# Who issues one plain weight transfer: GpSimd behind another one, or ACT

## The chip, the cores and the metric

The kernel runs on one core of one Trainium2 chip. The metric is the device time of one execution in microseconds (us): the median of several runs. Beside the timed runs there is one profiled execution, from which every row below comes; times in rows count from the start of its span.

## The reference

One decoder layer on a sequence of 512 tokens of width 1024, in float32: a SwiGLU half, a mixing block (a gated linear recurrence with 4 heads, and a gated short convolution), cross-attention into 256 memory rows, a second SwiGLU half and a last norm.

```
def swiglu(h, w_gate, w_up, w_down):
    return (jax.nn.silu(h @ w_gate) * (h @ w_up)) @ w_down
...
x = x + 0.5 * swiglu(rms_norm(x, ffn1_norm[l]), ffn1_gate[l], ffn1_up[l], ffn1_down[l])
...
x = x + 0.5 * swiglu(rms_norm(x, ffn2_norm[l]), ffn2_gate[l], ffn2_up[l], ffn2_down[l])
return rms_norm(x, final_norm)
```

The inner width of a SwiGLU half is 2816. The change touches only the products with w_gate and w_up, in both halves.

## The kernel before

Every float32 product is made of three: each operand is split into a high part, rounded for the fast multiply, and a low part, the rest. So each weight tile that comes from memory is first cast by ACT (`whi`, lines 100 and 312) and then subtracted by VectorE (`wlo`, lines 101 and 313), and TensorE (PE) multiplies high by high, high by low and low by high.

A SwiGLU half (class Half, used as f1 and f2) makes its 22 tiles of 128 inner columns in two ways. Tiles 0 to 3 (CLASSIC is 4) are made with plain products. From tile 4 on, tiles are made in pairs: gate and up weights of two tiles and the two halves of the input features and of the tokens form 2 x 2 blocks, and seven products take the place of eight (function seven). In the program's order the products are p1, p5, r6, p2, r7, p4, p3. The first three matter here. p1 multiplies the weight block b11 by the input block a11 into the PSUM tile psA. p5 multiplies t1 by q1 into psD. r6 first adds b22 to t1 (line 355), casts and splits that sum, and multiplies it by n2, on top of psA. Then p2 multiplies b21 into psB. Each of the products is 24 matmuls of 256 columns.

The five weight tiles of a pair are brought by load (line 287). Three are plain: b11, b22, b21. Two are sums of two blocks of the weights, made by the transfers themselves: t1 is first written plainly (line 300) and then a second transfer, which only GpSimd can issue, adds to it (line 301); t3 in the same way (lines 302 and 304). The adding transfer waits until the plain one has landed. All the tiles come from one pool of six buffers (tag raw), which the steps that prepare the inputs use too, so a transfer also waits until the last reader of its buffer is done. For t1 of the first pair that is n2l, the low part of n2 of the first tile pair (line 237).

The first pair (m equal to CLASSIC, once in each half) is loaded early, while the plain products' down projection (down_pairs, line 441) runs: line 466. There b11 goes out on GpSimd, t1's plain transfer on ACT and t3's plain transfer on SP; in later pairs b11 and t1 go out on SP and t3 on GpSimd.

The order of instructions on each engine isn't written out by hand: a scheduler takes the program, gives each instruction a place by its own estimate of when it could run, and then fixes one order for each engine. Each engine runs its list in order; GpSimd, SP and ACT issue transfers at the place where these stand in their list, and wait there for what the transfer needs.

In rows the names lose their ends: b_f is b11, b22 or b21; t_f is t1 or t3 (and a temporary of line 220); in_w is the weights; q1, n2, a11 with h or l are the parts of the inputs.

Of the kernel before, what the change touches and what calls it, by code (L numbers as in the profile page):

```python
# [38 lines left out]
def decoder_layer(ctx: ExitStack, tc: tile.TileContext, xT, memT, vecs, masks, ident_d,  # L39
                  w1, w1d, w_in, w_i, w_out, w_q, w_k, w_v, w_o, w2, w2d, gfin, out):  # L40
    nc = tc.nc
# [142 lines left out]
    CLASSIC = 4  # L184
    PARTS = ((0, 4), (4, 10), (10, 16), (16, FT))

    class Half:
# [99 lines left out]
        def load(self, m):  # L287


            def tile(key):  # L290
                return self.hp.tile([P, 2, 512], F32, tag="raw", name=f"{key}_{self.name}{m}", bufs=6)

            def src(j, h):
                return self.wgu[m:m + 2, j, :, h * 512:(h + 1) * 512].rearrange("m p c -> p m c")

            b11, t1, t3, b22, b21 = (tile(k) for k in ("b11", "t1", "t3", "b22", "b21"))

            queue = nc.gpsimd if m == CLASSIC else nc.sync
            queue.dma_start(b11, src(0, 0))
            (nc.scalar if m == CLASSIC else nc.sync).dma_start(t1, src(0, 0))  # L300
            nc.gpsimd.dma_start(t1, src(1, 0), accum_op=ALU.add)
            (nc.sync if m == CLASSIC else nc.gpsimd).dma_start(t3, src(1, 0))
            nc.sync.dma_start(b22, src(1, 1))
            nc.gpsimd.dma_start(t3, src(1, 1), accum_op=ALU.add)
            nc.sync.dma_start(b21, src(0, 1))
            return dict(b11=b11, t1=t1, b22=b22, b21=b21, t3=t3)
# [177 lines left out]
    with tc.tile_pool(name="start", bufs=1, reuse_waits="tile") as sp:  # L484
# [6 lines left out]
        for k0, k1 in steps:  # L491
            c = slice(k0 * P, k1 * P)
            src = w1[:2, :, :, c].rearrange("m j p c -> p (m j) c")
# [660 lines left out]
```

## Time and profile before

| | us |
|---|---|
| median of 3 runs | 1110.08 (1109.69 to 1110.9) |
| profiled execution | 1112.6 |
| its span, first to last instruction | 1110.8 |
| PE busy | 1093.6 (98%) |
| VectorE busy | 731.0 (66%) |
| ACT busy | 485.5 (44%) |
| GpSimd busy | 76.3 (7%) |

The busy time of an engine tells which engine the others have to keep fed; the waits tell where it wasn't. In a timeline row the first number is the start, the second the duration, and the bracket at the end holds the idle time of the engine before this instruction and what ended it. PE's matmuls overlap: the distance between starts is what one costs.

### The profile page before, as it was taken

To read this page: it belongs to the slowest core of one execution; us is meant where nothing else is said; L and a number is where in the kernel's file an instruction comes from. 1 tells how busy PE (TensorE), PEld (TensorE's weight loads), DVE (VectorE), ACT (ScalarE), POOL (GpSimd) and SP (SyncE) were. 2 spreads that over 40 slices of the span, in tenths; PEclk is the share of its full clock that TensorE was granted. 3 is DMA by queue.
4 is the path that set the end of the run, shared out by engine and by line. 5 is a ranking of instruction groups with operands and counts; after the bars stand their busy time and mean duration, and the time that the engine had idled before them with its cause. 6 is when DMAs were issued, how large, how long until landed. Compare 5 with 4: busy or idle time off the path is not lost. (4 is left out here: it accounts for less than half of the span.)

```text
span 1110.8 us, 15932 instructions
## 1 busy us (share of the span) xinstructions
PE 1093.6 (98%) x6522; PEld 978.4 (88%) x6522; DVE 731.0 (66%) x975; ACT 485.5 (44%) x662; POOL 76.3 (7%) x77
## 2 busy tenths in 40 slices
PE   7989999999999999999999999999999999999997
PEld 6879998998998888888889888888899989989995
DVE  6696755774667575885777556548967747755744
ACT  6344533552445343222454344435535524533553
POOL 1011100110100000000100000000011101100102
PEclk9999999999999999999999999999999999999999
DMA  6266664673623322322233424232757645755421
GB/s 232 74 186 184 180 165 124 172 172 109 172 52 107 107 95 68 104 76 86 67 114 114 134 78 124 83 95 76 200 149 180 168 124 133 201 152 154 96 76 76
DMA packets 69177, 140.53 MB, mean 127 GB/s; under 512 B 4880, under 2 KB 21264, under 8 KB 69104
## 3 DMA queue, kind: packets, MB, share of 16 engines
q1 hardware_dynamic: 53760, 105.92, 30.4%
q0 software_dynamic: 12944, 30.28, 13.6%
q10 hardware_dynamic: 2400, 3.31, 0.9%
q8 instruction: 51, 0.84, 0.3%
q14 instruction: 22, 0.18, 0.1%
HBM read 137.40 MB, written 2.10 MB: 126 GB/s over the span
## 5 line engine op out<-in xcount | busy, mean ns | idle before, releaser
L100 ACT ACTIVATE whi<-raw 128x1024 fp32r<-128x1024 f32 (+1 forms) x133 | 133.1, 1002 | 302.5 <-issue 68.7
L101 DVE TENSOR_TENSOR wlo<-raw,whi 128x1024 fp32r<-128x1024 f32 (+1 forms) x133 | 152.9, 1151 | 66.5 <-ACT whi L100 66.0
L312 ACT ACTIVATE whi<-b_f 128x1024 fp32r<-128x1024 f32 x72 | 76.4, 1061 | 111.9 <-issue 36.0
L313 DVE TENSOR_TENSOR wlo<-b_f,whi 128x1024 fp32r<-128x1024 f32 x72 | 88.2, 1224 | 44.9 <-ACT whi L312 43.5
L109 PE MATMUL psd_f<-al_f,whi 128*128 128x512 f32 x280 | 109.1, 390 | 0.0
L110 PE MATMUL psd_f<-ah_f,wlo 128*128 128x512 f32 x280 | 108.9, 389 | 0.0
L108 PE MATMUL psd_f<-ah_f,whi 128*128 128x512 f32 x280 | 108.3, 389 | 0.0
L313 DVE TENSOR_TENSOR wlo<-t_f,whi 128x1024 fp32r<-128x1024 f32 x54 | 66.1, 1224 | 40.3 <-ACT whi L312 40.3
L181 DVE SCALAR_TENSOR_TENSOR xall<-psd_f,xall 128x512 f32<-128x512 f32 x52 | 35.5, 690 | 76.5 <-PE psd_f L110 76.5
L312 ACT ACTIVATE whi<-t_f 128x1024 fp32r<-128x1024 f32 x54 | 57.0, 1056 | 55.8 <-issue 23.7
L110 PEld LDWEIGHTS psd_f<-ah_f,wlo 128*128 128x128 f32 x280 | 52.6, 188 | 11.0
L109 PEld LDWEIGHTS psd_f<-al_f,whi 128*128 128x128 f32 x280 | 52.6, 188 | 11.0 <-DVE al_f L227 0.3
L108 PEld LDWEIGHTS psd_f<-ah_f,whi 128*128 128x128 f32 x280 | 52.6, 188 | 10.8
L334 PE MATMUL psD_f<-q1h_f,whi 128*128 128x256 f32 x144 | 41.1, 285 | 4.0 <-ACT whi L312 4.0
L334 PE MATMUL psA_f<-a11h_f,wlo 128*128 128x256 f32 x144 | 41.8, 290 | 0.0
L334 PE MATMUL psA_f<-a11l_f,whi 128*128 128x256 f32 x144 | 41.7, 289 | 0.0
L334 PE MATMUL psA_f<-a11h_f,whi 128*128 128x256 f32 x144 | 41.7, 289 | 0.0
L334 PE MATMUL psD_f<-q1l_f,whi 128*128 128x256 f32 x144 | 40.9, 284 | 0.0
L334 PE MATMUL psD_f<-q1h_f,wlo 128*128 128x256 f32 x144 | 40.8, 284 | 0.0
L334 PE MATMUL psA_f<-a22h_f,whi 128*128 128x256 f32 x144 | 40.8, 283 | 0.0
L334 PE MATMUL psA_f<-n2h_f,whi 128*128 128x256 f32 x144 | 40.8, 283 | 0.0
L334 PE MATMUL psA_f<-n2l_f,whi 128*128 128x256 f32 x144 | 40.8, 283 | 0.0
(831 smaller groups left out, 3216.4 us busy)
## 6 DMA issues: line engine op xcount, KB each, us to landing
b_f<-in_w SPq DMA_DIRECT2D x52, 512.0 KB, 4.8
t_f<-in_w POOLq DMA_DIRECT2D x52, 512.0 KB, 5.9
raw<-in_w_in SPq DMA_DIRECT2D x24, 512.0 KB, 3.5
t_f<-in_w SPq DMA_DIRECT2D x18, 512.0 KB, 5.9
raw<-in_w1d SPq DMA_DIRECT2D x20, 384.0 KB, 3.1
raw<-in_w SPq DMA_DIRECT2D x12, 512.0 KB, 3.6
raw<-in_w2d SPq DMA_DIRECT2D x16, 384.0 KB, 3.4
raw<-in_w2d SPq DMA_DIRECT2D x10, 512.0 KB, 3.4
```

The lines of the kernel that those rows point to most:

```text
L100: nc.scalar.activation(hi[:, c], raw[:, c], AF.Copy)
L101: nc.vector.tensor_tensor(lo[:, c], raw[:, c], r32(hi[:, c]), ALU.subtract)
L108: nc.tensor.matmul(out, lhsT=wh, rhs=xh, start=first, stop=False)
L109: nc.tensor.matmul(out, lhsT=wh, rhs=xl, start=False, stop=False)
L110: nc.tensor.matmul(out, lhsT=wl, rhs=xh, start=False, stop=last)
L181: nc.vector.scalar_tensor_tensor(x[k], ps, scale, x[k], op0=ALU.mult, op1=ALU.add)
L312: nc.scalar.activation(hi, raw, AF.Copy)
L313: nc.vector.tensor_tensor(lo, raw, r32(hi), ALU.subtract)
L334: nc.tensor.matmul(o, lhsT=a[:, i, w], rhs=b, start=first and i == 0 and k == 0 and n == 0, stop=k == 3 and n == 2, skip_group_check=True)
```

## The change

One line of load: for the first pair of each half the plain transfer of t1 is issued by GpSimd, right behind b11's, instead of by ACT. For the other pairs the line does what it did.

```
             queue = nc.gpsimd if m == CLASSIC else nc.sync
             queue.dma_start(b11, src(0, 0))
-            (nc.scalar if m == CLASSIC else nc.sync).dma_start(t1, src(0, 0))
+            queue.dma_start(t1, src(0, 0))
             nc.gpsimd.dma_start(t1, src(1, 0), accum_op=ALU.add)
```

Since the scheduler sets the order, it moves other instructions too. On GpSimd, in the first half (b_f_606 is b11, t_f_607 is t1, t_f_608 is t3; line 300 is t1's plain transfer, 301 and 304 the adding ones of t1 and t3):

```order
 L141 TENSOR_TENSOR rst_f_276<-rs_f_274,mhalf 128x4
 L299 DMA b_f_606<-in_w 128x2x512
+L300 DMA t_f_607<-in_w 128x2x512
+L304 DMA t_f_608<-in_w 128x2x512
 L301 DMA t_f_607<-in_w 128x2x512
-L304 DMA t_f_608<-in_w 128x2x512
 L301 DMA t_f_862<-in_w 128x2x512
 L302 DMA t_f_863<-in_w 128x2x512
```

The adding transfer of t1 stood ahead of that of t3 and stands behind it now. It is the same in the second half.

On PE, in the first half, at the start of p1 and p5 (whi_707 and wlo_708 are the parts of b11, whi_738 and wlo_739 those of t1):

```order
 L334 MATMUL psA_f_706<-a11h_f_377,whi_707 128x256
 L334 MATMUL psA_f_706<-a11l_f_378,whi_707 128x256
-L334 MATMUL psD_f_737<-q1h_f_426,whi_738 128x256
-L334 MATMUL psD_f_737<-q1l_f_427,whi_738 128x256
 L334 MATMUL psA_f_706<-a11h_f_377,wlo_708 128x256
 L334 MATMUL psA_f_706<-a11h_f_377,whi_707 128x256
...
 L334 MATMUL psA_f_706<-a11l_f_555,whi_707 128x256
 L334 MATMUL psA_f_706<-a11h_f_554,wlo_708 128x256
+L334 MATMUL psD_f_737<-q1h_f_426,whi_738 128x256
+L334 MATMUL psD_f_737<-q1l_f_427,whi_738 128x256
 L334 MATMUL psD_f_737<-q1h_f_426,wlo_739 128x256
```

The first two products of p5 stood behind the first two of p1, and stand behind all 24 of them now.

On VectorE, in the second half, while the plain tiles are finished (u_f_7003 is the product of gate and up of tile 3, al_f_6909 the low part of it, wlo_7036 that of a down weight, a12l and d3l parts of the inputs):

```order
 L223 TENSOR_TENSOR u_f_7003<-ps_f_1_6955,rsb_f_6738 128x512
+L237 TENSOR_TENSOR a12l_f_7103<-xal_f_6649,a12h_f_7102 128x512
+L224 TENSOR_TENSOR u_f_7003<-u_f_7003,t_f_7000 128x512
 L101 TENSOR_TENSOR wlo_7036<-raw_7034,whi_7035 128x1024
-L224 TENSOR_TENSOR u_f_7003<-u_f_7003,t_f_7000 128x512
-L237 TENSOR_TENSOR a12l_f_7103<-xal_f_6649,a12h_f_7102 128x512
+L227 TENSOR_TENSOR al_f_6909<-u_f_7003,ah_f_6908 128x512
 L237 TENSOR_TENSOR d3l_f_7107<-c_f_6655,d3h_f_7106 128x512
-L227 TENSOR_TENSOR al_f_6909<-u_f_7003,ah_f_6908 128x512
 L237 TENSOR_TENSOR a22l_f_7111<-xah_f_6648,a22h_f_7110 128x512
```

The low part of the tile's product moved one place forward, ahead of d3l.

## Rows read from the trace of the kernel before

**Rows 1.** The page, busy us (share of the span) xinstructions of each engine
```profile
PE 1093.6 (98%) x6522; PEld 978.4 (88%) x6522; DVE 731.0 (66%) x975; ACT 485.5 (44%) x662; POOL 76.3 (7%) x77
```

**Rows 2.** Waits of PE: who waited, for whom: us in total, times, longest
```profile
PE psD_f L334 <- ACT whi L312: 4.0, 1, 4.0
...
PE psw L108 <- ACT yh1h L829: 0.5, 1, 0.5
```

**Rows 3.** Timeline of PE at the first pair of the first half
```profile
83.14 0.58 PE L334 MATMUL psD_f<-q1h_f,whi 128*128 128x256 f32 x1 [4.02 <-ACT whi L312]
...
83.74 0.41 PE L334 MATMUL psA_f<-a11h_f,wlo 128*128 128x256 f32 x1
...
88.43 0.38 PE L334 MATMUL psD_f<-q1h_f,wlo 128*128 128x256 f32 x1
...
91.16 0.28 PE L334 MATMUL psA_f<-n2h_f,whi 128*128 128x256 f32 x1
...
94.04 0.28 PE L334 MATMUL psB_f<-a12h_f,whi 128*128 128x256 f32 x1
```

**Rows 4.** Windows: length, busy of PE PEld DVE ACT POOL, PEclk, DMA share, GB/s
```profile
83.00:88.40 5.40, 5.26 (x24) 5.26 (x25) 3.68 (x3) 1.15 (x2) 0.00 (x0) 0.50 0.68 246
88.40:94.00 5.60, 5.60 (x48) 5.60 (x47) 3.59 (x3) 2.60 (x3) 1.90 (x2) 0.98 0.59 86
```

**Rows 5.** Timeline of ACT, the same place
```profile
69.24 0.39 ACTq L300 DMA_DIRECT2D t_f<-in_w  x1
...
82.03 1.06 ACT L312 ACTIVATE whi<-t_f 128x1024 fp32r<-128x1024 f32 x1 [6.73 <-DMA t_f<-in_w]
```

**Rows 6.** Timeline of GpSimd, the same place
```profile
74.06 1.25 POOL L301 DMA_DIRECT2D t_f<-in_w  x1 [12.08 <-ACT a22h_f L236]
76.62 1.20 POOL L304 DMA_DIRECT2D t_f<-in_w  x1 [1.31 <-DVE d3l_f L237]
```

**Rows 7.** DMA issues (KB each, us to landing) near 71.8, 74.1 and 76.6
```profile
t_f<-in_w SPq DMA_DIRECT2D x1, 512.0 KB, 4.3
...
t_f<-in_w POOLq DMA_DIRECT2D x1, 512.0 KB, 7.9
...
t_f<-in_w POOLq DMA_DIRECT2D x1, 512.0 KB, 9.1
```

**Rows 8.** Timeline of VectorE, the same place
```profile
61.73 0.68 DVE L237 TENSOR_TENSOR n2l_f<-qn_f,n2h_f 128x512 fp32r<-128x512 f32 x1
...
80.14 1.22 DVE L313 TENSOR_TENSOR wlo<-b_f,whi 128x1024 fp32r<-128x1024 f32 x1
...
83.12 1.23 DVE L313 TENSOR_TENSOR wlo<-t_f,whi 128x1024 fp32r<-128x1024 f32 x1 [1.76 <-ACT whi L312]
84.38 1.23 DVE L320 TENSOR_TENSOR t_f<-t_f,b_f 128x1024 f32<-128x1024 f32 x1
86.81 1.23 DVE L313 TENSOR_TENSOR wlo<-t_f,whi 128x1024 fp32r<-128x1024 f32 x1 [1.20 <-ACT whi L312]
```

**Rows 9.** Timeline of SP, the same place
```profile
71.76 0.38 SPq L302 DMA_DIRECT2D t_f<-in_w  x1
```

**Rows 10.** Landing times over the span: line 301 alone, then all transfers into t_f
```profile
DMA to landing us min/median/max: 5.5/5.9/7.9
...
DMA to landing us min/median/max: 3.4/5.9/9.9
```

**Rows 11.** GpSimd's DMA queue, 77 to 79.5, then 80 to 83: packets, MB, share
```profile
q0 software_dynamic: 226, 0.44, 110.2%
...
q0 software_dynamic: 203, 0.41, 74.2%
```

**Rows 12.** Timelines of GpSimd and ACT, first pair of the second half
```profile
800.17 1.20 POOL L304 DMA_DIRECT2D t_f<-in_w  x1 [5.15 <-DVE u_f L223]
...
815.21 1.06 ACT L312 ACTIVATE whi<-t_f 128x1024 fp32r<-128x1024 f32 x1 [4.38 <-PE psd_f L109]
```

**Rows 13.** Waits of PE's weight loads in the second half, 774 to 830
```profile
PEld psd_f L109 <- DVE al_f L227: 0.3, 1, 0.3
```

More of the change, by code (lines that the diff above doesn't have):

```diff
@@ L299, in load @@
             queue.dma_start(b11, src(0, 0))
-            (nc.scalar if m == CLASSIC else nc.sync).dma_start(t1, src(0, 0))
+            queue.dma_start(t1, src(0, 0))
             nc.gpsimd.dma_start(t1, src(1, 0), accum_op=ALU.add)
```

## The prediction

> **What bounds the kernel now.** Read the page first: TensorE (PE) is busy 1093.6 of 1110.8 us [rows 1]. So a change counts only where PE waits, or where its clock is low. The view of PE's waits then says how little that is: 4.0 us in one place, the first product on psD, which waits for ACT's whi; the next one is 0.5 us [rows 2]. That place is the first pair of the first half, and the changed line feeds it.
>
> The timeline of PE there shows three things [rows 3]. PE runs two products of psA (weights b11, high part), idles from 79.12 (83.14 - 4.02) to 83.14, and goes on with psD. Then 22 products take 83.74 to 88.43, 0.213 us each; later 24 take 91.16 to 94.04, 0.12 us each. The windows say why: granted clock 0.50 up to 88.4 and 0.98 after it [rows 4], so 1.2 GHz and then 2.4 GHz. The drop came after the idle, and the full level was back 5.5 us after PE resumed.
>
> Now look at what is waited for. ACT casts t1 to its high part at 82.03 [rows 5], 0.07 after t1's accumulating transfer landed: GpSimd issued that at 74.06 and it took 7.9 us [rows 6, 7], so L = 82.0. From that landing L to the end of the three products of this place (psA, psD, and n2 on psA) there is a fixed chain [rows 5, 8]: whi 1.06, wlo 1.23, the sum t1 + b22 1.23, its whi about 1.06 and its wlo 1.23, ready at 88.04, L + 6.1. n2 still needs 22 of its 24 products after that, 2.64 at 0.12, so the place could end at L + 8.75. PE leaves this place, starting psB, at 94.04 [rows 3], L + 12.1.
>
> **The change part by part.** ACT loses two DMA issues, one in each half. PE waits for none of ACT's work around them, so this is worth nothing by itself.
>
> GpSimd gets them. In the first half t1's plain transfer can be issued once n2l has read its slot, at 62.4 [rows 8], instead of 69.2 [rows 5]. Even with the longest landing of these tiles, 9.9 us [rows 10], it is there by 73. Nothing waits for it before 74, so being earlier is worth nothing either. What counts is the third edit, which the diff doesn't show but the order does: on GpSimd the accumulate into t3 now stands ahead of the accumulate into t1. GpSimd works in order, and t3's accumulate cannot start until t3's plain transfer has landed. SP issues that at 71.76 and it takes 4.3 us, so 76.06; GpSimd started at 76.62, 0.56 later, and was busy 1.2 us [rows 6, 7, 9]. So t1's accumulate goes out at 77.8 instead of 74.06, 3.8 us later, and behind another accumulate.
>
> When does it land? No row shows two accumulates 1.2 us apart, so I bound it. From below: the fastest accumulate of this line took 5.5 us [rows 10], giving 83.3. From above: the longest of these tiles' transfers took 9.9, and if a further 1.4 us of the first transfer are still ahead, 89.1. The nearest row is the second accumulate of the same place: issued 2.56 us behind the first, it took 9.1 [rows 7]. At 1.2 us behind, 1.36 us more of the first are ahead: 10.5, so 88.3. The packets say the same. GpSimd's queue moved 226 packets in 2.5 us when alone, 90 per us, and 203 in 3 us, 68 per us, when SP's loads shared the engines [rows 11]. The pair is 512 packets of 2 KB. Before, it started at about 76.7, so it had some 297 done by 80 and the rest by 83.2, and the landing came at 85.7 (76.62 + 9.1), 2.5 us after the last packet. Started 2.4 us later it has 81 done by 80, needs 6.3 us more, and lands at 88.8. Against both, t3's plain transfer no longer shares its time with t1's and may land up to 0.9 earlier (4.3 against a shortest 3.4 [rows 10]). I take 88.0.
>
> The other edit of order is on PE: all 24 products of psA now stand ahead of psD. Their low part is ready at 81.36 [rows 8], so PE idles 79.12 to 81.4 instead of to 83.1 and has the 22 left done by 84.0 (at 0.12) or 86.1 (at 0.213). This is a gain only if t1 is there by then, and by the estimate it is not.
>
> From 88.0 then: whi 88.1 to 89.1; PE's first two products of psD at 89.2; wlo ready 90.4; 22 products at the low level would take 4.7 us. I expect the low level, since PE idles again, from 84.0 to 89.2, longer than the 4.0 us after which it fell before. The full level returns 5.5 us after PE resumes, at 94.7, so psD ends at 94.9. The sum's wlo is ready at 94.1, so it isn't waited for; n2 takes 24 x 0.12 = 2.9 and ends at 97.8. Against 94.04 that is +3.8 us. With the clock kept, psD ends at 93.1, n2 waits for its wlo until 94.1 and ends at 96.8: +2.7.
>
> After that PE is the bound again, with nothing behind it that could take up the loss (0.5 us is the next wait), so it goes through to the end.
>
> In the second half the same inversion is on GpSimd: t3's accumulate at 800.17, t1's now behind it at 801.4 [rows 12]. Work that hides it: ACT casts t1 only at 815.21, when PE frees a buffer. With 11.3 us (9.9 + 1.4) it lands at 812.7, 2.5 us before it is wanted, so I cost it at 0; if that cover went, each us over would be a us of PE. The order of VectorE also moves there: al of the third tile comes earlier, for which PE's weight load waited 0.3 us [rows 13]. Bounds: nothing gained, 0.3 gained; I take -0.2.
>
> Sum: +3.8 - 0.2 = +3.6 us. The profiled execution took 1112.6 us for a span of 1110.8, so it would take 1116.2. The median of the runs is 1110.08, 2.5 below the profiled one, and I put the same difference on it: 1113.7.
>
> A rule that speaks against all this: the Trainium skill, DMA: Bandwidth & Descriptors, section Issuing engines are not separate DMA queues, says that transfers from ScalarE, SyncE and GpSimd end on the same 16 engines and interleave whichever engine issued them, so that the choice only moves issue time. By that rule alone the sum would be about 0 and the time 1110.1. The trace agrees that the engines are shared (90 against 68 packets per us [rows 11]), but not that only issue time moves: GpSimd sat until 76.62 for a landing with another transfer queued behind it in the new order.
>
> **The rivals.**
>
> First, the order of the two accumulates doesn't matter, because the DMA engines are full and the pair is finished when it was finished before, 85.7. For it: the packets of both are the same, and the engines are shared by all queues. Against it: GpSimd's queue starts 2.4 us later and its engines have nothing else of weight to do in that time. Then psD starts at 86.9 and n2 ends between 94.5 (clock kept, L + 8.75) and 95.5 (clock low for 5.5 us after 86.9, so that psD's 22 end at 92.6): +0.4 to +1.5, less 0.2, so 1110.3 to 1111.4, no change that can be told.
>
> Second, faster. t1's accumulate lands as fast as the fastest of its line, 5.5 us, at 83.3. Then psD follows psA without a second idle, the clock never falls, and n2 ends at L + 8.75 = 92.1 against 94.04: -2.0, with the second half -2.2, so 1107.9. It decides the sign when t1 lands before 85.3 (94.04 - 8.75). For it: PE's first idle ends 1.7 us earlier whatever happens. Against it: the 5.5 us is of a transfer alone, and here t3's is 1.2 us ahead with SP's loads beside it.
>
> Third, worse: the landing is at the upper bound, 89.1, and the clock returns only after n2 (24 products more at 0.213 instead of 0.12, 2.2 us), or the second half's t1 comes after 815.21. n2 ends at 99.1 to 101.3: +5 to +7, 1115 to 1117.
>
> That the moved transfer itself hurts, or helps, I rule out above: it lands before anyone asks.
>
> **How the numbers follow.** About 0.2% (2.2 us) is what a measurement of this kernel can tell from no change; the three runs before lie within 0.11%. Chances: my forecast, t1 landing between 86.8 and 89.1, 0.63, of which 0.06 (early landing and clock kept) is under 2.2 us; the first rival 0.22, nearly all within; the second 0.08, a quarter of it within; the third 0.07. So faster 0.06, same 0.29, slower 0.65. The range runs from the first rival's lower side, with 0.7 for the spread of the runs, 1109.6, to the landing's upper bound of 89.1 with the clock as I expect it (n2 ends at 98.9, +4.9, less 0.2: 1114.8), with 0.8 for that spread, 1115.6. The forecast's own range is 1111.4 (landing at 86.8, clock kept) to 1114.8.
>
> **What would show it.** Right: in the changed profile GpSimd's line 304 stands at 76 to 77 and its line 301 about 1.2 us later; ACT's cast of t1 starts at 87 to 89; PE has two idles there, about 2.3 us before psA's low part and 3 to 5 before psD; a granted clock of 0.50 falls on psD; psB starts at 96.5 to 98.5; from there on the two traces differ by a constant. Wrong: ACT's cast before 85.3, or one idle only, or a clock that never falls; then the gain of PE's new order stands and the first or second rival holds. A PE wait between 815 and 825 would mean the second half is not covered.

## The result and the profile after

The changed kernel takes 1116.01 us (median of four runs, 1115.70 to 1116.44), the kernel before beside it 1110.49 us (four runs, 1109.69 to 1111.23): ratio 1.0047, 95% interval 1.0035 to 1.0059. It is slower, by 5.5 us, and lies just outside the range on record. Its profiled execution took 1115.7 us for a span of 1113.9 us, against 1112.6 and 1110.8 us before: 3.1 us more. The place and the cause are those of the prediction. The number is not, and that the two comparisons give 5.5 and 3.1 us is the key to why.

The view of TensorE's (PE's) waits after, against [rows 2]; columns: who waited for whom, us in total, times, longest. In the first pair the one wait of 4.0 us has become three. The first row, PE's wait for its first weights at the program's start, is not in [rows 2] and was 4.7 us before, so the 4.0 us there was not the longest wait, and not the only one above 0.5 us; the change doesn't touch it.

```profile
PE ps_f L108 <- ACT whi_start L509: 4.3, 1, 4.3
PE psD_f L334 <- ACT whi L312: 4.2, 1, 4.2
PE psA_f L334 <- DVE wlo L313: 2.3, 1, 2.3
...
PE psD_f L334 <- DVE wlo L313: 0.5, 1, 0.5
```

GpSimd's timeline after, against [rows 6] (start, us, engine, line, what, idle before):

```profile
61.66 0.77 POOL L299 DMA_DIRECT2D b_f<-in_w  x1 [27.91 <-DVE c_f L275]
63.43 0.72 POOL L300 DMA_DIRECT2D t_f<-in_w  x1 [0.99 <-DVE n2l_f L237]
76.28 1.25 POOL L304 DMA_DIRECT2D t_f<-in_w  x1 [12.13 <-DVE a12l_f L237]
77.05 1.72 POOL L301 DMA_DIRECT2D t_f<-in_w  x1
```

t1's plain transfer is out at 63.4 us, six us earlier than before, and t1's accumulate (line 301) at 77.05 us, three us later, because t3's (line 304) is now in front and GpSimd has nothing to do for 12 us until that one may go. What it waits for is the landing of t3's plain transfer, not the VectorE split in the bracket: in all 14 profiles of this study line 304 starts 0.5 to 0.6 us behind that landing. Here SP issued the plain transfer at 72.14 us and it took 3.6 us, to 75.74 (SP's timeline, then line 302):

```profile
72.14 0.38 SPq L302 DMA_DIRECT2D t_f<-in_w  x1
...
DMA to landing us min/median/max: 3.6/3.6/3.6
```

t1's accumulate (line 301 in this window) took 10.7 us and landed at 87.75 us:

```profile
DMA to landing us min/median/max: 10.7/10.7/10.7
```

That is 5.8 us later than before (81.96): 3.0 because it was issued later, 2.8 because it took longer behind t3's (10.7 against 7.9). GpSimd's DMA queue in the stretches 78 to 82 and 83 to 87 us (packets, MB, share of the engines' time), against [rows 11]:

```profile
q0 software_dynamic: 272, 0.52, 78.5%
...
q0 software_dynamic: 268, 0.52, 71.5%
```

Two transfers of about 270 packets, one behind the other: t1's packets move when t3's are through. The Trainium skill, DMA: Bandwidth & Descriptors, section Two DMAs through the same engine are not ordered, says that within one queue of one DMA engine descriptors start in order; the two blocks agree. Between the blocks, from 82.0 to 82.9 us, GpSimd's queue moved nothing; the queue of the plain loads is the only one in the view there:

```profile
q1 hardware_dynamic: 113, 0.23, 89.5%
```

The same gap stands in the other four profiles with this order (a1, e2, e4 and e6 below, at most 6 of its packets in that stretch). What holds the queue there is open.

ACT's timeline, against [rows 5]:

```profile
87.88 1.06 ACT L312 ACTIVATE whi<-t_f 128x1024 fp32r<-128x1024 f32 x1 [12.12 <-DMA t_f<-in_w]
...
91.55 1.06 ACT L312 ACTIVATE whi<-t_f 128x1024 fp32r<-128x1024 f32 x1 [2.13 <-DVE t_f L320]
```

PE's, against [rows 3], and the windows, against [rows 4] (length; busy of PE, PEld, DVE, ACT, POOL; PEclk; DMA share; GB/s):

```profile
79.18 0.28 PE L334 MATMUL psA_f<-a11h_f,whi 128*128 128x256 f32 x1
...
81.86 0.39 PE L334 MATMUL psA_f<-a11h_f,wlo 128*128 128x256 f32 x1 [2.29 <-DVE wlo L313]
...
84.48 0.28 PE L334 MATMUL psA_f<-a11h_f,wlo 128*128 128x256 f32 x1
...
88.98 0.58 PE L334 MATMUL psD_f<-q1h_f,whi 128*128 128x256 f32 x1 [4.23 <-ACT whi L312]
...
94.52 0.28 PE L334 MATMUL psA_f<-n2h_f,whi 128*128 128x256 f32 x1
...
97.40 0.28 PE L334 MATMUL psB_f<-a12h_f,whi 128*128 128x256 f32 x1
```

```profile
82.00:84.70 2.70, 2.70 (x22) 2.55 (x22) 0.00 (x0) 0.00 (x0) 0.00 (x0) 1.00 1.03 245
89.00:93.60 4.60, 4.13 (x17) 3.84 (x18) 3.38 (x3) 2.42 (x3) 1.19 (x1) 0.50 0.35 45
```

The reader sees the forecast's picture: b11's 22 products run in the gap at full clock (2.4 GHz), the second idle stretch follows, and psD starts at half clock (1.2 GHz). From psA's first product to psB's it now takes 18.22 us (97.40 - 79.18); before it took 15.31 (94.04 - 78.73). The place costs 2.9 us more, and the program reached it 0.45 us later, a shift from the program's start (last section).

The rest of the program is a constant. Measured time less the start of psB lies between 1018.3 and 1018.8 us in every profile of this study where the products up to psB stand in these orders (the table below). The second half was covered, as said: t1's accumulate went out at 802.35 us there, and ACT took the tile at 818.12 us, after a wait for PE and not for the transfer.

```profile
802.35 1.73 POOL L301 DMA_DIRECT2D t_f<-in_w  x1
...
818.12 1.06 ACT L312 ACTIVATE whi<-t_f 128x1024 fp32r<-128x1024 f32 x1 [4.33 <-PE psd_f L109]
```

### The profile page after: what moved, and what is told of

It reads as the page before. It is cut to its first block, busy times and chain, and to the rows that moved or that the text cites. A ratio compares the mean times of both kernels' runs of the same rounds, so it can differ in the third digit from the quotient of the medians.

```text
span 1113.9 us, 15932 instructions
## 1 busy us (share of the span) xinstructions
PE 1094.2 (98%) x6522; PEld 978.6 (88%) x6522; DVE 730.9 (66%) x975; ACT 485.5 (44%) x662; POOL 77.9 (7%) x79
## 5 line engine op out<-in xcount | busy, mean ns | idle before, releaser
L181 DVE SCALAR_TENSOR_TENSOR xall<-psd_f,xall 128x512 f32<-128x512 f32 x52 | 35.5, 690 | 76.3 <-PE psd_f L110 76.2
L334 PE MATMUL psA_f<-n2h_f,wlo 128*128 128x256 f32 x144 | 40.8, 283 | 0.0
```

What stands on the lines that cost most here:

```text
L181: nc.vector.scalar_tensor_tensor(x[k], ps, scale, x[k], op0=ALU.mult, op1=ALU.add)
L334: nc.tensor.matmul(o, lhsT=a[:, i, w], rhs=b, start=first and i == 0 and k == 0 and n == 0, stop=k == 3 and n == 2, skip_group_check=True)
```

## The experiments

All numbers in one table: when GpSimd starts t1's accumulate, when ACT starts its cast of t1, when psA and psB start, and the time of that profiled execution (us); then the median of the kernel's timed runs, their number, and the ratio to the kernel before with its interval. In e8 and e9 two psB products stand ahead of n2, so psB's start can't be compared. In e1 and e8 t1 lands long before ACT is free for it.

| kernel | L301 | cast t1 | psA | psB | profiled | median (runs) | ratio, 95% |
|---|---|---|---|---|---|---|---|
| before | 74.06 | 82.03 | 78.73 | 94.04 | 1112.6 | 1110.49 (4) | |
| b0, before | 75.35 | 83.17 | 79.67 | 94.04 | 1112.51 | 1111.52 (12) | 1.0003 (0.9993 to 1.0013) |
| b1, before | 73.83 | 80.37 | 78.76 | 91.47 | 1109.91 | | |
| b2, before | 74.99 | 82.10 | 79.92 | 93.19 | 1111.63 | | |
| b3, before | 74.42 | 82.08 | 79.51 | 93.17 | 1111.98 | | |
| after | 77.05 | 87.88 | 79.18 | 97.40 | 1115.7 | 1116.01 (4) | 1.0047 (1.0035 to 1.0059) |
| a1, after | 77.04 | 87.29 | 79.03 | 96.73 | 1115.31 | 1115.31 (5) | 1.0038 (1.0024 to 1.0052) |
| e1 | 69.00 | 76.01 | 79.53 | 90.47 | 1108.89 | 1109.53 (11) | 0.9989 (0.9980 to 0.9998) |
| e2 | 77.40 | 87.66 | 79.32 | 99.47 | 1117.83 | 1117.83 (5) | 1.0065 (1.0053 to 1.0077) |
| e3 | 73.97 | 81.88 | 78.53 | 91.21 | 1109.66 | 1110.35 (11) | 0.9997 (0.9989 to 1.0006) |
| e4 | 76.96 | 88.70 | 79.19 | 97.47 | 1116.11 | 1116.11 (5) | 1.0043 (1.0030 to 1.0055) |
| e6 | 77.21 | 87.86 | 79.35 | 97.32 | 1115.71 | 1115.94 (5) | 1.0046 (1.0034 to 1.0058) |
| e8 | 68.06 | 74.91 | 78.43 | - | 1106.59 | 1106.55 (6) | 0.9964 (0.9952 to 0.9976) |
| e9 | 74.76 | 82.32 | 79.99 | - | 1111.92 | 1111.36 (11) | 1.0003 (0.9994 to 1.0012) |

The kernel before was run 76 times in these series, b0's twelve included: median 1110.92 us, 1108.71 to 1113.60.

**Which part of the change costs it: e1, e2, e3, e6.** The change does three things: GpSimd issues t1's plain transfer, t3's accumulate passes t1's on GpSimd, and psA's products pass psD's on PE. Four kernels take these apart.

e1, the changed kernel with the accumulates put back in order:

```
-            nc.gpsimd.dma_start(t1, src(1, 0), accum_op=ALU.add)
+            first = nc.gpsimd.dma_start(t1, src(1, 0), accum_op=ALU.add)
...
-            nc.gpsimd.dma_start(t3, src(1, 1), accum_op=ALU.add)
+            with tc.issue_after(first.ins): nc.gpsimd.dma_start(t3, src(1, 1), accum_op=ALU.add)
```

> The changed kernel, with t1's accumulate held ahead of t3's on GpSimd. The orders of TensorE, VectorE and ACT in the first pair are then those of the kernel before; only the issuer of t1's plain transfer differs. Theory (the accumulates' order is the cause): t1's accumulate goes out near 68 us and lands near 75 us, nothing of the pair waits for t1; TensorE idles only from 79.3 to 81.4 us for b11's low part; no fall of the clock; psB starts near 89.6 us, 4.4 us ahead of the kernel before's profile and 7.8 us ahead of the changed one's: 1107.5 to 1109 us. Rival (the order of the accumulates is not it, GpSimd's own extra issue or the crowd of transfers is): t1 lands as late as 82 us or later, 1110 us or more. Rival on the clock: the 2.1 us idle drops the clock after all, then psB near 92 us and 1110 us.

GpSimd's and PE's timelines of e1:

```profile
63.78 0.72 POOL L300 DMA_DIRECT2D t_f<-in_w  x1 [1.00 <-DVE n2l_f L237]
69.00 1.25 POOL L301 DMA_DIRECT2D t_f<-in_w  x1 [4.50 <-DMA t_f<-in_w]
77.59 1.20 POOL L304 DMA_DIRECT2D t_f<-in_w  x1 [7.34 <-DVE d3l_f L237]
```

```profile
82.21 0.39 PE L334 MATMUL psA_f<-a11h_f,wlo 128*128 128x256 f32 x1 [2.05 <-DVE wlo L313]
...
90.47 0.28 PE L334 MATMUL psB_f<-a12h_f,whi 128*128 128x256 f32 x1
```

Six us off the changed kernel (1115.79 over all its runs, below), by one accumulate put ahead of another: the wait for t1 is gone, only that for b11's low part is left, and the clock did not fall. PE's order went back with it, as expected, so this run doesn't part the two orders; e2 and e6 do. psB came 0.9 us later than I wrote, because the whole execution stands 0.8 us later: VectorE takes 18.41 us from n2l to b11's low part here (62.53 to 80.94 us) as in the kernel before (61.73 to 80.14).

So the moved transfer is not what hurts. Against the kernel before, e1 shows the moved transfer alone, both orders being the old ones, and there it helps: the plain transfer is out at 63.78 us instead of 69.24, and t1's accumulate, which waits for its landing, at 69.00 instead of 74.06. The kernel is about 1 us under the one before, at the edge of what these runs can tell, and half a microsecond over the times I had expected.

e2, the kernel before with the accumulates alone exchanged (in the first pair of each half; the plain transfer stays with ACT and PE's order stays):

```
-            nc.gpsimd.dma_start(t1, src(1, 0), accum_op=ALU.add)
+            add_t1 = lambda: nc.gpsimd.dma_start(t1, src(1, 0), accum_op=ALU.add); m == CLASSIC or add_t1()
...
-            nc.gpsimd.dma_start(t3, src(1, 1), accum_op=ALU.add)
+            first = nc.gpsimd.dma_start(t3, src(1, 1), accum_op=ALU.add)
...
+            with tc.issue_after(first.ins): m == CLASSIC and add_t1()
```

> The kernel before, t1's plain transfer still issued by ACT, with only the two accumulates of the first pair exchanged on GpSimd (t3's ahead of t1's). The orders of TensorE, VectorE and ACT stay those of before, so two psD products that need t1 stand behind psA's second product. Theory: t1's accumulate goes out near 77.5 us and lands near 88 us; TensorE waits for it from 79.3 us to 89 us with 22 psA products behind the wait, low clock afterwards, psB near 100 us: 6 us later than in the kernel before, 2.6 us later than in the changed kernel, 1116 to 1119 us. Rival (what costs is that GpSimd issues the plain transfer, not the order): t1 lands near 82 to 84 us and the time is that of the kernel before within 1.5 us.

PE's timeline of e2:

```profile
88.76 0.58 PE L334 MATMUL psD_f<-q1h_f,whi 128*128 128x256 f32 x1 [9.05 <-ACT whi L312]
...
99.47 0.28 PE L334 MATMUL psB_f<-a12h_f,whi 128*128 128x256 f32 x1
```

One wait of 9 us with all of psA's rest behind it: 2.0 us more than the changed kernel, where 2.6 was expected.

e3, the kernel before with PE's order alone changed: in the first pair psD's products are issued behind psA's last one.

```
-                multiply("D", st["raw"]["t1"], "q1", True)
+                with tc.issue_after(st["mm"].ins) if m == CLASSIC else nullcontext(): multiply("D", st["raw"]["t1"], "q1", True)
```

> The kernel before with only TensorE's order changed: all 24 psA products of the first pair stand ahead of the first psD product, as in the changed kernel; issuers and the accumulates' order as before. Theory: TensorE idles 79.3 to 81.4 us for b11's low part, runs psA's 22 products at full clock to about 84.1 us, meets t1's cast already made (83.1 us), psB near 91 us, 3 us ahead of the kernel before's profile: 1108 to 1110 us. This is the part of the change that by itself helps; if the place in the kernel before usually costs less than its profile shows (the clock kept there), the gain against the median is only about 0.7 us. Rival (the products' order is worth nothing, since t1 ends the wait in both): psB near 94 us, no change of the time.

psB came at 91.2 us, where theory had it, but the median is 0.3 us under the kernel before, which can't be told from nothing. What the order buys is the long end: e3's eleven runs reach 1110.76 us, and 14 of the 29 runs of the kernel before in the same series took longer than that. PE's timeline gives a likely reason why it is no shorter in the usual case (not tested by itself): the clock fell behind its one idle stretch too, and the products after that took 0.21 us.

```profile
81.21 0.39 PE L334 MATMUL psA_f<-a11h_f,wlo 128*128 128x256 f32 x1 [2.28 <-DVE wlo L313]
...
82.55 0.41 PE L334 MATMUL psA_f<-a11h_f,wlo 128*128 128x256 f32 x1
```

e6 is e2 and e3 together: everything that the change does, except who issues the plain transfer.

> The kernel before, t1's plain transfer still issued by ACT, with both things that the changed kernel has besides: t3's accumulate ahead of t1's on GpSimd, and all 24 psA products ahead of psD on TensorE. Theory (the issuer itself costs nothing, these two orders are the whole change): t1's accumulate goes out near 77 us, its cast starts near 87.5 us, psB about 9.5 us after that cast, near 97 us, as in the changed kernel: 1115 to 1116.5 us; 2 us less than with the inversion alone. Rival (issuing the plain transfer on GpSimd has a price of its own, such as its 0.7 us of issue time ahead of the others): 1 us or more below the changed kernel, under 1114.5 us.

1115.94 us, psB at 97.32 us: the changed kernel again. With t3's accumulate in front, who issues the plain transfer is worth nothing; the two orders are the whole change, the first costs about 7 us (e2 against the kernel before), and the second gives about 2 of them back (e6 against e2). With t1's accumulate in front it is worth about 1 us (e1 against the kernel before), since the accumulate then waits for the plain transfer alone. The rule of the Trainium skill that I weighed against the change (DMA: Bandwidth & Descriptors, section Issuing engines are not separate DMA queues) says that issuing from several engines saves only the time on the sequencer; e6 against the changed kernel, 0.15 us, agrees for the moved transfer itself. The 5 us come from an issuing engine that stands in front of a wait, with another transfer behind it.

**Why 5.5 us by the runs and 3.1 by the profiles: b0 to b3, a1.** These are the kernels before and after, unchanged.

> The kernel before, unchanged, profiled once more. It tells where the gap of the two medians (1110.5 to 1116.0, +5.5 us) and the gap of the two profiled executions (1112.6 to 1115.7, +3.1 us) part. Theory A: the profiled execution of before was a late one of its kind; in the usual ones TensorE's clock does not fall at the 4 us idle before psD, 24 products at 0.21 us instead of 0.12 us, so they are shorter by about 2.3 us: this profile shows 1.00 of full clock through 83 to 94 us, psB near 91.7 us, 1109.7 to 1111.2 us. Theory B (rival): the place is the same in every execution (psB near 94.0 us, clock at half for 83 to 88 us) and the 2.1 us lie elsewhere, at the program's start or end or between profiled and unprofiled executions: then the profile shows psB 15.3 us after the first psA product whatever the total. Theory C: t1's accumulate lands earlier than 82.0 us in most executions: idle before psD 2 us instead of 4.

> The kernel before, unchanged, one more profile, to see what differs between its executions. Theory: the time follows psB (time minus psB start is 1018.5 us in every profile so far, within 0.3 us); an execution at 1109 to 1110 us has psB at 90.5 to 91.5 us because t1's accumulate lands 1 to 3 us earlier and the clock does not fall or falls late. Rival: psB is near 94 us in every execution and the shorter ones are shorter elsewhere.

> As the run before it: one more profile of the kernel before. If its time is within 0.5 us of 1112.5 us, psB is near 94.0 us; if it is near 1109.5 us, the theory says psB near 91 us, the rival says 94 us.

> The kernel before, unchanged, a fifth profile. By the others its time is the start of psB plus 1018.5 us within 0.3 us, and psB is 11 to 12 us behind the start of ACT's cast of t1, which starts 6.5 to 8.0 us after GpSimd issues the accumulate. A fixed place and a varying rest would speak against that.

> The changed kernel, unchanged, profiled and timed once more beside the kernel before. Its four times so far lie within 0.8 us (1115.7 to 1116.4), those of the kernel before within 4.7 us (1108.9 to 1113.6). Theory (what varies in the kernel before is the landing of t1's accumulate and with it the fall of the clock; the changed kernel waits longer than that in every execution): times stay between 1115 and 1117 us, psB 18 us after the first psA product, clock at half on psD. Rival (four times were luck): a spread of 4 us or more, median near 1114 us, which would bring the difference of the medians to that of the profiles, 3.1 us.

PE's timeline and ACT's in b1, the short execution, against [rows 3] and [rows 5]:

```profile
81.48 0.39 PE L334 MATMUL psD_f<-q1h_f,whi 128*128 128x256 f32 x1 [2.33 <-ACT whi L312]
...
88.59 0.28 PE L334 MATMUL psA_f<-n2h_f,whi 128*128 128x256 f32 x1
...
91.47 0.28 PE L334 MATMUL psB_f<-a12h_f,whi 128*128 128x256 f32 x1
```

```profile
80.37 1.06 ACT L312 ACTIVATE whi<-t_f 128x1024 fp32r<-128x1024 f32 x1 [5.03 <-DMA t_f<-in_w]
```

B falls: the kernel before has no fixed place. Theory C holds, the landing varies. Theory A is wrong about the clock, which fell in all five profiles, in the short b1 too; what varies is for how long:

```profile
82.10:85.40 3.30, 3.30 (x18) 3.30 (x17) 2.06 (x3) 1.06 (x1) 0.00 (x0) 0.50 1.04 376
```

b2 and b3 lie between the two cases that I had named for b2 (1111.63 and 1111.98 us, psB at 93.2 in both). From the start of the accumulate to the cast it takes 8.0, 7.8, 6.5, 7.1 and 7.7 us in its five profiles, and psB follows the cast by 10.9 to 12.0 us (the first profile, the one I worked from, has 12.0, with half clock on every product from 83 to 88.4 us; in b0 half of that stretch was at full clock):

```profile
84.30:87.20 2.90, 2.90 (x13) 2.90 (x14) 2.41 (x2) 0.34 (x1) 0.00 (x0) 0.50 1.08 287
87.20:91.00 3.80, 3.80 (x34) 3.80 (x33) 1.93 (x2) 2.26 (x3) 0.00 (x0) 1.00 0.40 150
```

From psA to psB: 15.31, 14.37, 12.71, 13.27, 13.66 us. The median time of the 76 runs, 1110.92, less 1018.5 puts the usual psB at 92.4 us. The execution on which I had built was at the late end of its kernel (70 of the 76 runs were shorter), and late in just the landing and the clock that the change replaces: against the mean of the four later profiles it took 0.7 us more from accumulate to cast (7.97 against 7.28) and 1.0 us more from cast to psB (12.01 against 11.04), while its accumulate started 0.6 us earlier. The changed kernel's nine runs have a median of 1115.79 us, which puts psB at 97.3; its two profiles have 18.22 and 17.70 us from psA to psB. So the difference is 4.9 us by the runs (1115.79 - 1110.92). The means of the profiles give 17.96 - 13.86 = 4.1 us for the place. The 0.8 us between the two is no more than one execution's start-up shifts (last section), and with five profiles against two it was not followed further.

The repeated runs of the changed kernel spread more than expected (1113.62 to 1116.42); the rival of 4 us or more did not come.

**What the clock costs in the changed kernel: e4.** 32 extra products fill PE's second idle stretch; the line is called where psD's bank is taken, in the first half.

```
+            def keep_clock(count):
+                for _ in range(count):
+                    with tc.issue_after(st["mm"].ins):
+                        nc.tensor.matmul(st["D"][:, 0], lhsT=st["wA"][0][:, 0, :P], rhs=self.q["a11"][0][0][:, 0], start=True, stop=False, skip_group_check=True)
```

> The changed kernel with 32 extra products of 256 columns on TensorE between psA's last product and psD's first, in the place of its second idle stretch (they write into psD's bank, whose first real product starts it anew; the result is unchanged). 32 at 0.12 us fill 3.8 of the 4.2 us. Theory: t1's cast still ends near 89 us and the wait stays, but psD's products now run at 0.12 us instead of 0.21 us: psB near 95.3 us instead of 97.4 us, time 2.1 us less, about 1114 us. That is what the clock's fall costs in the changed kernel; the rest, against 1109.5 us without the wait, is the wait. Rival (the fall of the clock is not caused by that idle stretch, or VectorE's wlo of t1 and of the sum set the pace): psB near 97 us, no change.

The windows and PE's timeline of e4:

```profile
84.70:89.90 5.20, 5.20 (x38) 5.20 (x37) 0.11 (x1) 1.20 (x2) 0.00 (x0) 0.81 0.79 248
89.90:97.40 7.50, 6.23 (x50) 5.82 (x49) 6.25 (x6) 3.31 (x4) 1.19 (x1) 1.00 0.42 71
```

```profile
91.08 0.39 PE L334 MATMUL psD_f<-q1h_f,wlo 128*128 128x256 f32 x1 [0.74 <-DVE wlo L313]
94.74 0.39 PE L334 MATMUL psA_f<-n2h_f,wlo 128*128 128x256 f32 x1 [0.53 <-DVE wlo L313]
...
97.47 0.28 PE L334 MATMUL psB_f<-a12h_f,whi 128*128 128x256 f32 x1
```

The clock had fallen behind the first idle stretch, was back before the landing and stayed at 1.00, and the 2.1 us did not come; my theory here falls. psB follows the cast by 8.77 us, where it was 9.52 in the changed kernel (9.44 in a1, 9.46 in e6): by this one execution the low clock costs about 0.7 us, and then the chain of casts and sums behind t1 is the bound, with a new wait for VectorE's low part of the sum (0.53 us). The prediction had that chain (landing + 8.75); in this expectation I forgot it. In this execution t1 also landed 0.8 us later, and the median of e4's runs (1116.11) is no lower than the changed kernel's, so the times show nothing of the 0.7 us.

**A version that beats both: e8, and its half, e9.** e1 leaves PE waiting for b11's low part, which stands on VectorE behind eight splits of the inputs. Two of these (a22) are wanted only by the pair's sixth product. e8 is e1 with them moved; e9 is the kernel before with the same edit alone.

```
-                if len(steps) == 8:
+                if len(steps) == 6:
...
-            begin(steps + later, lambda: self.finish(3, p3))
+            a22 = [later.pop(6), later.pop(4)][::-1]; begin(steps + later, lambda: self.finish(3, p3))
...
-                r6()
+                r6(); [s() for s in a22]; a22 = []
```

> The changed kernel with t1's accumulate held ahead of t3's on GpSimd, and the two a22 splits of the inputs moved behind the first pair's third unit in the program, so that b11's low part is made on VectorE before them. With the accumulate early, what TensorE waited for was b11's low part (2.05 us) and then nothing, while VectorE had no idle time from 60 to 84.5 us. Theory (VectorE sets the pace there): b11's low part is ready by 79 us, psA and psD run without idle from 79.5 to 85.3 us, the sum's split follows about 1.2 us earlier; the end comes 1 to 2 us earlier than with the accumulate alone: 1107.3 to 1108.5 us. Rival (the delayed a22 splits or b21's transfer are late for the fourth and sixth products and take the time back): 1109.5 us, as without it.

> The kernel before with only the two a22 splits moved behind the first pair's third unit in the program; issuers and the accumulates' order as before. The scheduler then also moves one of the two early psD products behind psA's. Theory (two waits stand one behind the other: b11's low part until 81.4 us, and t1's landing until 80.4 to 83.2 us; taking away only the first leaves the second): TensorE still waits for ACT's cast of t1 at 80 to 83 us, psB 91 to 94 us, 1110 to 1111.5 us, the time of the kernel before within 0.7 us. Rival (the a22 splits by themselves give the 2 to 3 us that the combined version has over the accumulate alone): 1108 us or less.

VectorE's timeline of e8 (b11's low part, then t1's) and PE's:

```profile
77.23 1.22 DVE L313 TENSOR_TENSOR wlo<-b_f,whi 128x1024 fp32r<-128x1024 f32 x1
80.17 1.22 DVE L313 TENSOR_TENSOR wlo<-t_f,whi 128x1024 fp32r<-128x1024 f32 x1
```

```profile
78.43 0.28 PE L334 MATMUL psA_f<-a11h_f,whi 128*128 128x256 f32 x1
...
81.30 0.28 PE L334 MATMUL psD_f<-q1h_f,whi 128*128 128x256 f32 x1
...
85.28 0.39 PE L334 MATMUL psB_f<-a12h_f,whi 128*128 128x256 f32 x1 [0.44 <-ACT whi L312]
```

And PE's wait in e9:

```profile
83.43 0.39 PE L334 MATMUL psD_f<-q1h_f,whi 128*128 128x256 f32 x1 [3.04 <-ACT whi L312]
```

e8 runs psA and psD without a gap and takes 1106.55 us, 4 us less than the kernel before and 9 less than the changed one, a little more than expected. Between the profiles of e1 and e8, 1.1 us of the difference is the start of psA, which e9 with the same edit has at 79.99 us (a shift from the program's start, last section), and 1.2 the place. The medians lie 3.0 us apart, more than the place explains; where the rest comes from is open. The same edit without the early accumulate (e9) gives nothing: b11's low part is ready at 80.0 us there, and PE waits for t1 until 83.4 us.

## Why the prediction was right on the place and wrong on the time

- The inversion on GpSimd, its reason and its times: right. Line 304 at 76.3 us (said: 76 to 77), line 301 behind it, 0.77 us later (said: 1.2). e1 and e2 show that this order is the cause: put into the kernel before it adds 7 us (e2), put right in the changed kernel, with PE's order going back, it takes 6 off (e1).
- "Nothing waits for it before 74, so being earlier is worth nothing either", said of t1's plain transfer: wrong. GpSimd's accumulate at 74.06 was itself waiting for it. It was issued at 69.24 and took 4.2 us, so it landed at 73.44, 0.6 us ahead; the bracket in [rows 6] names an ACT split. In e1 the earlier transfer lets the accumulate out 5 us earlier. In the changed kernel the inversion hides this.
- t1's landing, taken as 88.0: 87.75 us. That it came so near is in part luck: the issue was 0.75 us earlier than said (77.05 against 77.8) and the transfer 0.5 us longer than the 10.2 behind the 88.0. The reckoning by packets took one unbroken stream and 2.5 us from the last packet to the landing. The runs show a gap of about 0.9 us between the two transfers, and in the kernel before GpSimd's queue still moved packets from 83.2 to 85.7 us, where the prediction had it done:

```profile
q0 software_dynamic: 35, 0.04, 9.6%
```

- PE's two idle stretches (2.3 and 3 to 5 us), half clock on psD, psB at 96.5 to 98.5: 2.29 and 4.23 us, 0.50, 97.40. In a1 the second stretch was 2.46 us, below what was said, because the clock had fallen while psA's products ran; psB came at 96.73 all the same. In the trace of before the clock did not drop after the idle stretch, as the prediction reads it, but in it: it was at 0.50 from 82 to 83 us, while PE still stood idle.
- The price of the low clock, +3.8 against +2.7 without: 1.1 said, about 0.7 by e4's profile.
- The second half at no cost: right; that it would be 0.2 faster was of the size that can't be told.
- The sum against the profiled execution, 1116.2: the changed kernel's profile had 1115.7, its runs a median of 1115.79.
- The step that failed is the last: "The median of the runs is 1110.08, 2.5 below the profiled one, and I put the same difference on it". The 2.5 us were no property of profiling (the profiled executions of e1 and e3 are among the shortest of their kernels). 0.8 of them was the median of three runs lying below that of the 76 (1110.08 against 1110.92). The rest sat in the place that the change rebuilds (psB at 94.04 against the usual 92.4): in the landing of 7.9 us, which [rows 10] shows as the longest of its line (5.5, 5.9 and 7.9), and, for the larger share, in the length of the half clock. b1, whose accumulate took 1.4 us less, is 2.7 us shorter. The changed kernel waits for another landing, so nothing of the 2.5 was its due. Taking psB before at its usual 92.4 us and after at 97.8, less 0.2, gives +5.2; measured were +5.5, and +4.9 over all runs.
- The range inherited the error: its upper end, 1114.8 and 0.8 for spread, was made from the same subtraction. The 0.7 and 0.8 for spread came from three runs; the 76 lie 4.9 us apart.
- Rival one (the accumulates' order doesn't matter) fell with e2; rival two (faster) needed t1 by 85.3 us, and it landed at 87.75. Rival three has the time (1115 to 1117) but not the mechanism: the landing was not at the bound, the clock was back before n2, and the second half was covered.

## What to carry to other kernels

Before a sum on one profile is carried to the median of the runs, ask where the profile's own excess sits: if the wait that the change replaces is the one that was long in this execution, the excess goes with it. A line of landing times with its spread can hint at it: the wait at its maximum is a suspect. Here it pointed at the smaller share, and only more profiles of the unchanged kernel told how long its clock is usually low. And a transfer that waits on an engine whose list is worked in order holds back all that stands behind it there (GpSimd stood for 12 us here), so a changed issuer is judged by the order in which the engine gets its work, not by the edit.

## What was not expected of the hardware

- The granted clock at the program's start differs between executions of one kernel. The windows of 8 to 16 us, of the kernel before in its first profile and in b2 (columns as above):

```profile
8.00:16.00 8.00, 5.59 (x18) 4.51 (x19) 6.13 (x9) 6.89 (x11) 0.00 (x0) 1.00 1.03 416
```

```profile
8.00:16.00 8.00, 5.04 (x13) 3.98 (x14) 5.58 (x9) 6.33 (x11) 0.00 (x0) 0.57 1.04 418
```

  With the fall psA starts at 79.0 to 80.0 us (ten profiles), without it at 78.4 to 78.8 (four): about 0.8 us.
- The same length of idle time did not always have the same result: behind 2.05 us in e1 and 2.29 us in the first profile of the changed kernel PE ran on at full clock; behind 2.28 us in e3 and the same 2.29 us in a1, the changed kernel again, the clock fell within 1.2 us of PE going on (a1, where PE went on at 81.71 us). Why is open.

```profile
81.90:82.70 0.80, 0.80 (x8) 0.80 (x8) 0.00 (x0) 0.00 (x0) 0.00 (x0) 1.00 1.00 323
82.90:85.90 3.00, 3.00 (x15) 2.75 (x13) 0.00 (x0) 0.00 (x0) 0.00 (x0) 0.50 1.08 233
```

- The landing of the same accumulate varied between 6.4 and 7.9 us over five profiles of the kernel before, with t3's 2.1 to 2.8 us behind it; issued early, with nothing else in its queue, it took 6.7 (e1) and 6.5 us (e8), and right behind t3's 10.1 to 11.6 us (five profiles). What makes the longer ones long was not tried.
